# Moving the 8 KB buffer class of a two-block transformer kernel by 64 bytes

## The chip, the cores and the metric

The kernel runs on one core of a Trainium2 chip. The metric is the device time of one execution in microseconds; three runs of the kernel before gave 1069.27 us as median (1068.24 to 1070.73).

## The reference

Two transformer layers follow each other, with 512 tokens and 1024 features in float32. The first has a differential attention (4 heads) and a sparse attention with three branches (8 heads, 2 key-value heads): a compressed one, a selected one and a windowed one. The second has a short convolution, an attention over the 256 keys that an indexer picks, and a gated feed-forward layer (FFN) of width 2816.

```python
def reference(x, norm_g, w_in, ..., g_final_2):
    x = first_block(x, norm_g, w_in, ...)
    return second_block(x, g_mix_2, w_in_2, ...)

# second_block, its end
merged = gates[..., :D_MODEL] * y_a + gates[..., D_MODEL:] * y_b
x = x + merged @ w_out[layer]
h2 = rms_norm_2(x, g_ffn[layer])
x = x + (jax.nn.silu(h2 @ w_ffn_gate[layer]) * (h2 @ w_ffn_up[layer])) @ w_ffn_down[layer]
return rms_norm_2(x, g_final)
```

## The kernel before

Every dense product is made of three float32r matmuls: an operand is split into a rounded part and the rest (hi and lo), and hi by hi, hi by lo and lo by hi are summed in PSUM (`mm3`, line 169). A matmul reads two operands from SBUF: the stationary one is loaded into the array by a weight load (PEld in the profile), and the moving one is streamed through, 128 to 512 columns of 4 bytes per partition. The weight load of the next matmul overlaps the matmul before it. In the profile's names, `acc<-hT,whi` has hT as the moving and whi as the stationary operand.

The products come in two forms. In `gen_ii` and `gen_tt` a piece of the activation (hT, act, mg, oTd, oTn) is stationary and the weight moves, 256 to 512 columns at a time; in `gen_i` and in the FFN's first product (`Pair.product`) a piece of the weight is stationary and the activation moves (hT, yc, at with 512 columns, hA with 256). The FFN's first product is done with seven half-size products in place of eight (the sums `S1` to `S4` of the activations, and sums of the weights), and between these products a few steps of the second product are put (`feed_forward`, line 1416). Attention's dependent chains are spread out by due times (`defer`, `fill`), so that dense matmuls stand between the steps; the order of all instructions is written out when the program is built.

All tiles live in one SBUF pool. Each class of buffers (a tag, with a number of buffers) gets its room when its first tile is asked for, in that order, and each room is rounded up to 32 bytes per partition. The classes are `kf` (3 buffers of 4 KB), `k4` (13 of 4 KB), `k2` (19 of 2 KB), `k8` (13 of 8 KB), `sm` (28 of 96 bytes) and `kh` (4 of 512 bytes); a constant is a class of one buffer. Weights, raw and split, lie in `kf`, `k4` and `k2`, and so do probabilities, transposed probabilities and values; the activations that are operands of dense products, in hi and lo, lie in `k8`, and so do queries and keys, X, and the split weights of the first FFN products (`split_of` with `early`).

Four built-in constants and a 4 KB scratch area end at byte 4224, which is 16 x 256 + 128. `kf`, `k4` and `k2` follow (3 x 4096, 13 x 4096 and 19 x 2048 bytes), so that every buffer of theirs begins at 128 modulo 256. Then, before, come mhalf (32), identF (512), sm (28 x 96 = 2688), identR (512) and ones (32): 108672 + 3776 = 112448, which is 64 modulo 256. So every buffer of `k8` begins at 64 modulo 256, 64 bytes short of the phase of `k4` and `k2`; all pieces that a matmul reads lie at multiples of 512 bytes inside their buffer. identF, the identity that moves in transposes of float32, lies at 160 modulo 256, and identR, that of float32r, at 32.

```python
def t(self, cls, shape, dt=F32, name="w"):
    return self.pool.tile(shape, dt, name=name, tag=cls, bufs=BUFS[cls])

def const(self, shape, name, dt=F32):
    return self.pool.tile(shape, dt, name=name, tag="c_" + name, bufs=1)
```

Of the kernel before, what the change touches and what calls it, by code (L numbers as in the profile page):

```python
# [9 lines left out]
F32 = mybir.dt.float32  # L10
# [5 lines left out]
P = 128  # L16
# [31 lines left out]
class Kernel:  # L48
# [26 lines left out]
    def t(self, cls, shape, dt=F32, name="w"):  # L75
        return self.pool.tile(shape, dt, name=name, tag=cls, bufs=BUFS[cls])
# [104 lines left out]
    def tick(self):  # L181
        c, self.cost = getattr(self, "cost", 0.0), 0.0
        if self.filling and not self.busy:
            self.credit -= c
        self.spend(c)
# [66 lines left out]
def build(tc, pool, psum, dram, h):  # L252
    nc = tc.nc
    K = Kernel(tc, pool, psum, dram, h)
    t, ps, defer, tick = K.t, K.ps, K.defer, K.tick
# [15 lines left out]
    S, MAKE = Lazy(), {}  # L271
# [10 lines left out]
    def f32(ap):  # L282
        return ap.bitcast(F32)
# [108 lines left out]
    def new_hT():  # L392
        return [[t("k8", [P, 4, T], F32R, "hT") for _ in range(2)] for _ in range(2)]
# [26 lines left out]
        return f  # L420


    xin = [t("kf" if tt < 3 else "k4", [P, D], F32, "xt") for tt in range(NT)]
    gB1 = t("k4", [P, D], F32, "gB")

    def x_load(tt):
        for c in range(XP):
            a = slice(c * D // XP, (c + 1) * D // XP)
            S["x"] = tc.keep_in_program_order(nc.sync.dma_start(xin[tt][:, a], x[tt * P:(tt + 1) * P, a])).ins

    grow = t("k2", [P, P], F32, "grow")[0:8]
    nc.scalar.dma_start(grow, h["norm_g"][0].rearrange("(r c) -> r c", c=P))
    x_load(0)

    mhalf = K.const([P, 1], "mhalf")
    V.memset(mhalf, -0.5)
    identF = K.const([P, P], "identF")
    make_identity(nc, identF)
# [15 lines left out]
        K.tr(warm, gB1[:, b * P:(b + 1) * P], identF)  # L454
    identR = K.const([P, P], "identR", F32R)
    G.tensor_copy(identR, identF)
    ones = K.const([P, 1], "ones")
    V.memset(ones, 1.0)


    S["hT"] = new_hT()

    NV = 65
    maskc = K.const([P, T], "maskc")
    DM = K.const([P, T], "DM")
    cmask = K.const([P, 4, 32], "cmask")
    rowok = K.const([P, 1], "rowok")
    qsc = K.const([P, 4, 2, 4], "qsc")
    cw2 = K.const([P, 2, 2, 64], "cw2")
    rbT = K.const([8, 32], "rbT")  # L470
    rel_rows = dram.tile([8, 640], F32, name="rel_rows")
# [1 line left out]
    vec = K.const([P, NV], "vec")  # L473
    GD = K.const([P, 64], "GD")
    GN = K.const([P, 3, 64], "GN")
    c01 = K.const([P, 2], "c01")

    def constants():
        vrow = t("k2", [P, P], F32, "vrow")
# [337 lines left out]
        return evac  # L817


    KC = K.const([P, 64], "KC")  # L820

    def cmp_evac(m, o):
        v = m % 2
# [68 lines left out]
    def cmp_finish():  # L892
        for v in range(2):
# [5 lines left out]
            if v == 0:  # L899
# [12 lines left out]
                def go(kd=kd):  # L912
                    pk = ps([P, 64], name="pt")
                    K.tr(pk, kd[0:64].rearrange("p a d -> p (a d)"), identF[0:64, 0:64])
                    A.copy(KC, pk)
                    tick()
# [18 lines left out]
    def cmp_attention(g):  # L935
        st = {}

        def rows(tt):
            sc = ps([P, 4, 32], name="sc")
            for c in range(4):  # L940
                K.mm(sc[:, c, :], f32(S["nQ%d" % g][:, c, tt * P:(tt + 1) * P]), KC[:, g * 32:(g + 1) * 32],
                     c == 0, c == 3)
# [718 lines left out]
def emit(tc, h, stage="all"):  # L1661
    with tc.tile_pool(name="sb", bufs=1) as pool, \
            tc.tile_pool(name="ps", bufs=1, space=bass.MemoryType.PSUM) as psum, \
            tc.tile_pool(name="dr", bufs=1, space=bass.MemoryType.DRAM) as dram, \
            contextlib.nullcontext():
        build(tc, pool, psum, dram, h)
# [18 lines left out]
```

## Time and profile before

| | |
|---|---|
| median of three runs | 1069.27 us |
| the profiled execution | 1069.85 us |
| its span, first to last instruction | 1068.1 us |
| mean granted TensorE clock | 0.996 |
| matmuls / weight loads | 7251 / 7251 |
| PE, PEld busy | 1045.6 us (98%), 963.6 us (90%) |
| VectorE, ScalarE, GpSimd busy | 717.8, 556.2, 398.5 us |
| DMA, mean over the span | 103 GB/s |

The times of the profile are those of one execution. A matmul's recorded end is modelled and lies behind the start of the next one, so that the length of one matmul in a row says little, and a busy PE is not one that works at its peak. What can be read exactly is the start: the pitch, the time from the start of one matmul to the start of the next, is taken from two starts of the timeline and the number of matmuls between them. A few records of matmuls can be missing.

### The profile page before, as it was taken

How to read it: one execution, taken by the hardware profiler on the slowest of the kernel's cores; microseconds unless marked ns; L12 is line 12 of the kernel's file. 1: busy time of each engine (PE TensorE's matmuls, PEld its weight loads, DVE VectorE, ACT ScalarE, POOL GpSimd, SP SyncE). 2: the span in 40 equal slices, each digit the busy share in tenths (PEclk: the TensorE clock that was granted, in tenths of full speed). 3: DMA queues.
4: the chain of work that ended last, by engine and by line, in shares of the span. 5: the costliest groups of instructions: out<-in, count | busy, mean ns of one | idle time of the engine just before them, and what ended most of it. 6: DMA issues, size and time to landing. Idle time of an engine off the chain costs nothing.

```text
span 1068.1 us, 18962 instructions
## 1 busy us (share of the span) xinstructions
PE 1045.6 (98%) x7251; PEld 963.6 (90%) x7251; DVE 717.8 (67%) x1469; ACT 556.2 (52%) x1154; POOL 398.5 (37%) x403
## 2 busy tenths in 40 slices
PE   7999999999999999999999999999999999999997
PEld 6999898899789899888888888989999999999995
DVE  6777467346993637999313663979887777777724
ACT  5566687647883445523323776426444444444433
POOL 4442366465466231112015975910012112121241
PEclk9999999999999999999999999999999999999999
DMA  6446321221204434435331323651433323333122
GB/s 184 124 110 161 79 61 40 73 86 41 79 21 148 139 82 159 115 82 168 99 98 53 88 88 100 227 158 54 145 109 119 119 76 104 92 116 109 31 90 79
DMA packets 128085, 109.69 MB, mean 103 GB/s; under 512 B 20393, under 2 KB 119154, under 8 KB 127994
## 3 DMA queue, kind: packets, MB, share of 16 engines
q1 hardware_dynamic: 126906, 105.83, 33.8%
q0 software_dynamic: 1072, 2.65, 0.6%
q8 instruction: 57, 0.93, 0.4%
q14 instruction: 34, 0.28, 0.1%
q10 hardware_dynamic: 16, 0.00, 0.0%
HBM read 103.13 MB, written 6.84 MB: 103 GB/s over the span
## 4 chain that ended last, share of the span: by engine, by line
PE 88%; DVE 5%; DMA 2%; POOL 2%; ACT 2%; issue 1%; SPq 0%; POOLq 0%; DVEq 0%; ACTq 0%
PE acc L164 75%; PE pt L178 5%; PE sc L164 4%; PE o L164 4%; POOL wlo L208 1%; DMA xt<-in_x 1%; ACT p L637 1%; DMA raw<-in_w_ffn_up 1%; DVE p L635 1%; DVE acc L1550 0%; POOL mg L1214 0%; DVE mg L1217 0%; DMA raw<-in_w_out 0%; DVE wlo L208 0%; DVE hA L1402 0%
## 5 line engine op out<-in xcount | busy, mean ns | idle before, releaser
L208 POOL TENSOR_TENSOR wlo<-raw,whi 128x1024 fp32r<-128x1024 f32 (+4 forms) x99 | 205.1, 2077 | 443.5 <-ACT whi L206 343.7
L164 PE MATMUL acc<-hA,wh 128*128 128x256 f32 x1264 | 219.5, 280 | 1.8 <-ACT wh L1273 1.8
L206 ACT CAST whi<-raw 128x1024 fp32r<-128x1024 f32 (+4 forms) x143 | 131.9, 924 | 125.5 <-PE acc L164 80.1
L164 PE MATMUL acc<-hT,whi 128*128 128x512 f32 x608 | 194.4, 398 | 0.0
L164 PEld LDWEIGHTS acc<-hA,wh 128*128 128x128 f32 x1264 | 190.3, 190 | 2.4 <-ACT wh L1273 2.0
L164 PE MATMUL acc<-whi,hT 128*128 128x256 f32 (+3 forms) x896 | 181.2, 291 | 2.0 <-ACT whi L206 1.9
L164 PE MATMUL acc<-hA,wl 128*128 128x256 f32 x584 | 163.1, 280 | 0.0
L164 PEld LDWEIGHTS acc<-whi,hT 128*128 128x128 f32 x896 | 144.4, 189 | 3.3 <-ACT whi L206 2.2
L164 PEld LDWEIGHTS acc<-hT,whi 128*128 128x128 f32 x608 | 112.2, 188 | 24.5 <-ACT r L1549 0.2
L164 PE MATMUL acc<-wlo,hT 128*128 128x256 f32 (+3 forms) x448 | 129.4, 289 | 0.9 <-DVE wlo L208 0.9
L164 PE MATMUL acc<-whi,act 128*128 128x256 f32 (+1 forms) x640 | 130.0, 289 | 0.0
L164 PE MATMUL acc<-hT,wlo 128*128 128x512 f32 x304 | 120.9, 398 | 0.0
L164 PEld LDWEIGHTS acc<-hA,wl 128*128 128x128 f32 x584 | 110.3, 189 | 0.0
L164 PEld LDWEIGHTS acc<-whi,act 128*128 128x128 f32 x640 | 104.0, 188 | 2.5
L164 PE MATMUL acc<-wlo,act 128*128 128x256 f32 (+1 forms) x320 | 92.3, 289 | 0.0
L637 ACT ACTIVATE p<-p,s 128x128 f32<-128x128 f32 (+3 forms) x128 | 72.1, 565 | 32.0 <-DVE s L635 28.9
L1273 ACT CAST wh<-raw 128x1024 fp32r<-128x1024 f32 x55 | 57.6, 1051 | 55.2 <-PE acc L164 45.7
L164 PEld LDWEIGHTS acc<-wlo,hT 128*128 128x128 f32 x448 | 84.7, 189 | 1.4 <-DVE wlo L208 1.1
L1274 DVE TENSOR_TENSOR wl<-raw,wh 128x1024 fp32r<-128x1024 f32 x51 | 63.3, 1243 | 31.4 <-PE acc L164 17.3
L208 DVE TENSOR_TENSOR wlo<-raw,whi 128x1024 fp32r<-128x1024 f32 (+5 forms) x44 | 53.5, 1217 | 41.7 <-ACT whi L206 41.5
L164 PEld LDWEIGHTS acc<-hT,wlo 128*128 128x128 f32 x304 | 57.2, 188 | 13.1
L164 PEld LDWEIGHTS acc<-wlo,act 128*128 128x128 f32 x320 | 60.1, 188 | 1.3
(283 smaller groups left out, 2038.7 us busy)
## 6 DMA issues: line engine op xcount, KB each, us to landing
raw<-in_w_in SPq DMA_DIRECT2D x52, 512.0 KB, 3.9
raw<-in_w_ffn_gate SPq DMA_DIRECT2D x28, 512.0 KB, 3.9
raw<-in_w_ffn_up SPq DMA_DIRECT2D x22, 512.0 KB, 5.2
raw<-in_w_ffn_down SPq DMA_DIRECT2D x36, 256.0 KB, 5.3
raw<-in_w_out SPq DMA_DIRECT2D x16, 512.0 KB, 3.4
raw<-in_cmp_w SPq DMA_DIRECT2D x8, 512.0 KB, 3.7
raw<-in_w_in SPq DMA_DIRECT2D x10, 384.0 KB, 3.4
rel_all<-rel_rows POOLq DMA_DIRECT2D x1, 2560.0 KB, 17.2
```

Source lines behind the costliest of these rows:

```text
L164: self.nc.tensor.matmul(out, lhsT, rhs, start=start, stop=stop, skip_group_check=True)
L178: self.nc.tensor.transpose(out, in_, ident)
L206: self.nc.scalar.copy(hi, raw)
L208: (self.nc.gpsimd if every and self.split and self.split % every == 0 else self.nc.vector).tensor_tensor(lo, raw, hi.bitcast(F32), op=OP.s ...
L635: V.tensor_tensor_reduce(out=p[:, :n], in0=sc[:, :n], in1=bias, scale=-scale, scalar=3e38, op0=OP.add, op1=OP.min, accum_out=nm)
L637: S["exp"] = A.activation(p[:, :n], p[:, :n], AF.Exp, scale=-1.0, bias=nm, accum_out=z).ins
L1273: A.copy(hi, src)
L1274: eng.tensor_tensor(lo, src, f32(hi), op=OP.subtract)
```

## The change

Lines that ask for constants are put in another order, and `S["hT"]`, the first use of `k8`, is asked for earlier. Behind `k2` now comes `qsc` alone (4 x 2 x 4 floats, 128 bytes), then `k8`: 108672 + 128 = 108800, which is 0 modulo 256. So every buffer of `k8` begins at 0 modulo 256, 128 bytes from the phase of `k4` and `k2`, where it was 64. Behind `k8` come mhalf, ones, rowok, c01 (32 bytes each), KC (256), identF, sm and identR, and the constants that came later. identF now lies at 128 modulo 256, identR at 0, KC at 128 (32 before), the masks maskc, DM and cmask at 0 (64 before). `kf`, `k4`, `k2` and `kh` stay where they were.

No engine's sequence changes: each of the five has the same instructions with the same operands, waits and signals in the same order; only addresses in SBUF differ.

```diff
     xin = [t("kf" if tt < 3 else "k4", [P, D], F32, "xt") for tt in range(NT)]
     gB1 = t("k4", [P, D], F32, "gB")
+    grow = t("k2", [P, P], F32, "grow")[0:8]
+    qsc = K.const([P, 4, 2, 4], "qsc")
+    S["hT"] = new_hT()
+    mhalf, ones = K.const([P, 1], "mhalf"), K.const([P, 1], "ones")
+    rowok, c01 = K.const([P, 1], "rowok"), K.const([P, 2], "c01")
+    KC = K.const([P, 64], "KC")
...
-    grow = t("k2", [P, P], F32, "grow")[0:8]
     nc.scalar.dma_start(grow, h["norm_g"][0].rearrange("(r c) -> r c", c=P))
     x_load(0)
 
-    mhalf = K.const([P, 1], "mhalf")
     V.memset(mhalf, -0.5)
...
-    ones = K.const([P, 1], "ones")
     V.memset(ones, 1.0)
 
-
-    S["hT"] = new_hT()
...
-    rowok = K.const([P, 1], "rowok")
-    qsc = K.const([P, 4, 2, 4], "qsc")
...
-    c01 = K.const([P, 2], "c01")
...
-    KC = K.const([P, 64], "KC")
```

## Rows read from the trace of the kernel before

**Rows 1.** The page: busy time of each engine over the span with the number of instructions (its part 1), and the shares of the chain of work that ended last, by engine (its part 4).

```profile
PE 1045.6 (98%) x7251; PEld 963.6 (90%) x7251; DVE 717.8 (67%) x1469; ACT 556.2 (52%) x1154; POOL 398.5 (37%) x403
...
PE 88%; DVE 5%; DMA 2%; POOL 2%; ACT 2%; issue 1%; SPq 0%; POOLq 0%; DVEq 0%; ACTq 0%
```

**Rows 2.** Groups of instructions by line on PE, of the whole span: line, engine, operation, output<-moving operand, stationary operand, shape, count | busy us, mean ns of one (with its modelled end) | idle time before. Only the counts are used. In the names, whi and wlo are the two halves of a weight tile (4 KB class, or 2 KB class for the FFN's second product), wh and wl those of the FFN's first product, hT, hA, act, at, yc, mg and oTd are activations (8 KB class).

```profile
L164 PE MATMUL acc<-hA,wh 128*128 128x256 f32 x1264 | 219.5, 280 | 1.8 <-ACT wh L1273 1.8
...
L164 PE MATMUL acc<-hA,wl 128*128 128x256 f32 x584 | 163.1, 280 | 0.0
...
L164 PE MATMUL acc<-whi,act 128*128 128x256 f32 (+1 forms) x640 | 130.0, 289 | 0.0
...
L164 PE MATMUL acc<-wlo,act 128*128 128x256 f32 (+1 forms) x320 | 92.3, 289 | 0.0
...
L164 PE MATMUL acc<-whi,hT 128*128 128x256 f32 (+3 forms) x896 | 181.2, 291 | 2.0 <-ACT whi L206 1.9
...
L164 PE MATMUL acc<-wlo,hT 128*128 128x256 f32 (+3 forms) x448 | 129.4, 289 | 0.9 <-DVE wlo L208 0.9
...
L164 PE MATMUL acc<-whi,mg 128*128 128x256 f32 (+1 forms) x192 | 43.4, 318 | 0.5 <-DVE mg L1217 0.5
...
L164 PE MATMUL acc<-wlo,mg 128*128 128x256 f32 (+1 forms) x96 | 29.9, 317 | 0.1
...
L164 PE MATMUL acc<-whi,oTd 128*128 128x256 f32 x128 | 23.8, 281 | 0.0
...
L164 PE MATMUL acc<-wlo,oTd 128*128 128x256 f32 x64 | 17.8, 279 | 0.0
...
L164 PE MATMUL acc<-hT,whi 128*128 128x512 f32 x608 | 194.4, 398 | 0.0
...
L164 PE MATMUL acc<-hT,wlo 128*128 128x512 f32 x304 | 120.9, 398 | 0.0
...
L164 PE MATMUL acc<-at,whi 128*128 128x512 f32 x64 | 20.1, 395 | 0.0
...
L164 PE MATMUL acc<-at,wlo 128*128 128x512 f32 x32 | 12.5, 395 | 0.0
...
L164 PE MATMUL acc<-yc,whi 128*128 128x512 f32 x64 | 20.1, 396 | 0.0
...
L164 PE MATMUL acc<-yc,wlo 128*128 128x512 f32 x32 | 12.7, 396 | 0.0
...
L178 PE MATMUL pt<-identF,p 128*128 128x128 f32 x280 | 46.6, 275 | 1.3 <-POOL p L1024 0.8 <-DVE PTb L654 0.3
...
L178 PE MATMUL pt<-identF,xn 128*128 128x128 f32 x88 | 12.9, 287 | 1.3 <-DVE xn L1473 1.3
```

**Rows 3.** Timeline of PE in the FFN: start in us, length in us with the modelled end, engine, line, operation, names, shape, count. Between the first row and the second lie 24 matmuls, between the second and the third 12, then 24, then 18.

```profile
879.47 0.40 PE L164 MATMUL acc<-hA,wh 128*128 128x256 f32 x2
...
882.20 0.28 PE L164 MATMUL acc<-whi,act 128*128 128x256 f32 x1
...
883.56 0.40 PE L164 MATMUL acc<-hA,wh 128*128 128x256 f32 x2
...
886.39 0.28 PE L164 MATMUL acc<-whi,act 128*128 128x256 f32 x1
...
888.52 0.40 PE L164 MATMUL acc<-hA,wh 128*128 128x256 f32 x2
```

**Rows 4.** Timeline of PE, same columns, at the FFN's start, behind the last of the row blocks. Each row of acc<-hA,wl follows two matmuls of acc<-hA,wh; from the first row to the second there are thirteen such triples, 39 matmuls.

```profile
733.21 0.28 PE L164 MATMUL acc<-hA,wl 128*128 128x256 f32 x1
...
737.63 0.28 PE L164 MATMUL acc<-hA,wl 128*128 128x256 f32 x1
```

**Rows 5.** Timeline of PE, same columns: 48 matmuls in which the weight tile (wh) is of the 8 KB class too, and the 12 transposes behind them.

```profile
714.66 5.92 PE L164 MATMUL acc<-hA,wh 128*128 128x256 f32 x48
720.41 1.47 PE L178 MATMUL pt<-identF,xs 128*128 128x128 f32 x12
721.72 0.60 PE L178 MATMUL pt<-identF,xn 128*128 128x128 f32 x4
```

**Rows 6.** Timeline of PE, same columns, in the first projection: 256 columns of a weight move against a stationary piece of hT. From the first row to the second there are ten triples, 30 matmuls.

```profile
212.21 0.28 PE L164 MATMUL acc<-wlo,hT 128*128 128x256 f32 x1
...
215.74 0.28 PE L164 MATMUL acc<-wlo,hT 128*128 128x256 f32 x1
```

**Rows 7.** Timeline of PE, same columns, in the second block's projection: 512 columns of hT move against a stationary piece of a weight. From the first row to the second there are seven triples, 21 matmuls.

```profile
530.84 0.40 PE L164 MATMUL acc<-hT,wlo 128*128 128x512 f32 x1
...
535.74 0.39 PE L164 MATMUL acc<-hT,wlo 128*128 128x512 f32 x1
```

**Rows 8.** Timeline of PE, same columns, in the last product: 512 columns of a weight move against a stationary piece of act. From the first row to the second there are 30 matmuls.

```profile
1038.95 0.39 PE L164 MATMUL acc<-wlo,act 128*128 128x512 f32 x1
...
1045.82 0.39 PE L164 MATMUL acc<-wlo,act 128*128 128x512 f32 x1
```

**Rows 9.** Stretches of the span: bounds in us, length, PE busy and its matmuls, granted clock, DMA share and GB/s.

```profile
732.00:768.00 36.00, 34.20 (x284) 0.95 0.44 132
800.00:1000.00 200.00, 200.00 (x1729) 1.00 0.33 100
```

**Rows 10.** Groups of instructions by line on VectorE, of the whole span: an addition that reads PSUM and a tile of the 8 KB class (X), and one that reads PSUM and a tile of the 2 KB class (part).

```profile
L1074 DVE TENSOR_TENSOR X<-acc,X 128x512 f32<-128x512 f32 x56 | 37.9, 682 | 18.6 <-PE acc L164 18.3
...
L1348 DVE TENSOR_TENSOR gu<-acc,part 128x512 f32<-128x512 f32 x33 | 22.5, 683 | 3.9 <-ACT part L1343 2.8 <-PE acc L164 1.2
```

## Prediction, made before the changed kernel was run

> **What bounds the kernel now.** I read the page first: PE is busy for 1045.6 of 1068.1 us, and the chain of work that ended last is PE for 88% of its length, DVE for 5%, everything else for 7% [rows 1]. So the time is the number of matmuls times their pitch, and only what alters the pitch can alter it by much. Since no engine's sequence changes, what is to be asked is whether the pitch hangs on where operands lie. The second view is therefore the timeline of PE, read by starts alone, for the same shape with operands of different classes. Three things are to be seen there.
>
> First, matmuls of one shape do not have one pitch. 256 columns of hA (8 KB class) against a weight of the 4 KB class take (737.63 - 733.21)/39 = 113.3 ns in one stretch [rows 4]. In the middle of the FFN the same instructions take 2.73/24 = 113.8 ns in one product and 2.83/24 = 117.9 ns in the next; the steps of the second product between them keep the pace of the product ahead of them, 1.36/12 = 113.3 and 2.13/18 = 118.3 ns [rows 3]. PE waits for nothing there, the granted clock is 1.00, and 200 us of this hold 1729 matmuls, 115.7 ns each [rows 9], the middle of the two paces.
>
> Second, the one stretch in which both operands are of the 8 KB class, so begin at the same phase modulo 256, is the slowest of this shape: 5.75/48 = 119.8 ns [rows 5].
>
> Third, direction counts. With 512 columns, hT moving against a weight takes 4.90/21 = 233.3 ns [rows 7], a weight moving against act 6.87/30 = 229.0 ns [rows 8]. In the first the stationary operand lies 64 bytes behind the moving one (modulo 256), in the second 64 bytes ahead. With 256 columns and hT stationary the pitch is 3.53/30 = 117.7 ns [rows 6].
>
> My reading is that the stream of the moving operand and the load of the next weights get in each other's way in SBUF, at worst with equal phases, and by more or less at a distance of 64 depending on which of them is ahead. The trace of before has no steady stretch of dense matmuls at a distance of 128. So what follows is an extrapolation along the distance 0, 64, 128.
>
> **The change part by part.** The distance between the 8 KB class and the weights goes from 64 to 128, in both directions. I take the cleanest pace seen as the bound from below (113.3 ns for 256 columns, twice that, 226.6, for 512) and the equal-phase pace as the bound from above (119.8; 233.3 for 512, the slowest row). Counts are those of [rows 2].
>
> - 512 columns with the 8 KB class moving: 608 + 304 (hT) + 64 + 32 (at) + 64 + 32 (yc) = 1104, now at 233.3. At the nearest row that is better, 229.0, this gives 1104 x 4.3 = 4.7 us; at 226.6 it gives 7.4.
> - FFN, 256 columns: 1264 + 584 (hA) and 640 + 320 (act), of which 96 have 512 columns (the last product: 4 row blocks x 2 halves x 4 pieces x 3). Of the 2712 left, 284 are in the stretch that is clean already [rows 9], and 96 have weights of the 8 KB class, whose distance stays 0. 2332 x (115.7 - 113.3) = 5.6 us.
> - A weight moving against hT, mg or oTd: 896 + 448, 192 + 96 less 96 of 512 columns, 128 + 64, in all 1728 of 256 columns or a little more: 1728 x (117.7 - 113.3) = 7.6 us.
> - The 192 of 512 columns among act and mg: 192 x (229.0 - 226.6) = 0.5 us, or nothing.
> - Scores (query by key, both in the 8 KB class) and probabilities by values (both in the smaller classes) keep their distance 0: nothing.
>
> The sum lies between 17.9 and 21.1 us; I take 19.5. Not all of it arrives: where PE waits for a softmax chain or for a GpSimd subtraction, a faster PE waits longer. 12% of the chain is not PE's [rows 1], so I count 88%: 17.2 us.
>
> identF moves to the phase of p and xn, the data that its transposes load as weights: distance 0 where it was 32. The 280 + 88 transposes take 1.31/12 = 109.2 ns now (the same form, with xs) [rows 2, 5]. If they pay what the equal phase costs above, 119.8 - 113.3 = 6.5 ns, that is 2.4 us; since the trace shows no second distance for them, a gain of the same size can't be excluded. I take a third of the cost, 0.8 us.
>
> Other homes that change: X on VectorE. Its addition takes 682 ns with the 8 KB class at 64 and 683 with a tile of the 2 KB class at 128 [rows 10]; that engine doesn't mind, and I count masks and small tiles at nothing. Were VectorE slower by the same 5% as PE between its paces, it would still have a third of the span free.
>
> So 1069.85 - 17.2 + 0.8 = 1053.4 us for an execution like the profiled one. That one lay 0.6 above the median of the runs: 1053 us (rounded). The likeliest case by itself reaches from 1047 (all of 21.1 us and nothing lost) to 1058 (half of the third term and of the first missing).
>
> [...]
>
> **The rivals.**
>
> *Half of it: the two paces stay.* In the FFN the pace flips where the second product's steps give way to the next half-size product, with the same classes on both sides [rows 3]. So distance alone doesn't fix the pace; something that is carried along does, perhaps how far the weight load trails the stream. Then the 256-column matmuls may go on flipping at distance 128, and only hT, at and yc with 512 columns gain: 4.7 x 0.88 = 4.1 us, 1065. Against it: the flip comes just where the last weight that moves and the next stationary weight are both of the small classes, distance 0, and none comes within a product.
>
> *No effect.* Homes don't matter to PE, and the paces come from something else, such as what the other engines do meanwhile: 1069. For it: that the paces flip with homes unchanged. Against it: the 39 matmuls at 113.3 ns [rows 4] run beside VectorE and ScalarE work of the same kind, and the equal-phase stretch has no pace but 119.8.
>
> *Slower: the pattern repeats every 128 bytes.* Then a distance of 128 is a distance of 0, and all dense matmuls pay what the 48 of [rows 5] pay. Price: 2332 x (119.8 - 115.7) = 9.6; the 284 clean ones 284 x 6.5 = 1.8; 1728 x (119.8 - 117.7) = 3.6; the 192 of 512 columns 192 x (233.3 - 229.0) = 0.8; 15.8 us together, all of it on PE's chain: 1069.85 + 15.8 - 0.6 = 1085 us. For it: in the FFN the plus-64 and the minus-64 direction share one pace, fast or slow [rows 3], which a period of 128 would make equal by itself. Against it: with 512 columns the two directions differ, 233.3 against 229.0 [rows 7, 8], which it would not. It decides from the point at which products of hA against a 4 KB weight average more than 116 ns.
>
> **How the numbers follow.** The clean case 0.52, half of it 0.15, no effect 0.13, slower 0.20. About 0.2% is what a measurement of this kernel can tell from no change. Faster takes the first two, 0.67; within 0.2% 0.13; slower 0.20. The predicted time is that of the likeliest case, 1053 us. The range reaches from 1045 (the whole 21.1 us and a gain on the transposes) over the half case and no effect to 1076, the near half of the slower case, which leaves most of that case's 0.20 outside and little below. The clean case's own range is 1047 to 1058.
>
> **What would show it.** Right: in the FFN every product at 113 to 114 ns, so some 1760 matmuls between the bounds of 200 us where 1729 stand now [rows 9]; hT with 512 columns at 229 or less; the 48 matmuls with both operands of the 8 KB class still at 119.8 ns, since their distance is unchanged; VectorE's, ScalarE's and GpSimd's mean durations as before. A gain that is smaller with the paces as predicted would show as more idle time ahead of PE, behind softmax chains and GpSimd's wlo. The transposes of identF at 109 ns would put their term at nothing. Wrong: paces that still flip between 113 and 118 (half of it), the same mixture as before everywhere (no effect), or 119 to 120 for all of the FFN and no 512-column pitch under 233 (slower).

## The result and the profile after

The changed kernel is slower: 1077.51 us as median of four runs (1077.27 to 1077.77) against 1069.83 (1068.24 to 1070.73) for the kernel before in the same measurement, a ratio of 1.0076 with a 95% interval of 1.0060 to 1.0092. Forecast were 1053 us and a range of 1045 to 1076: the sign is wrong, and the time lies 1.5 us above the range.

The page of after, its busy times and its chain, which answer to [rows 1]:

```profile
span 1075.7 us, 18962 instructions
...
PE 1054.1 (98%) x7251; PEld 971.9 (90%) x7251; DVE 717.5 (67%) x1469; ACT 556.0 (52%) x1154; POOL 398.9 (37%) x403
...
PE 89%; DVE 5%; DMA 2%; ACT 2%; issue 1%; POOL 0%; SPq 0%; POOLq 0%; DVEq 0%; ACTq 0%
```

The span grew by 7.6 us and PE's busy time by 8.5, with the same 7251 matmuls; the other three engines have what they had, within 0.4 us. So the question is the pitch, and the matmuls of [rows 3 to 8] are looked up again. First the FFN, the same five matmuls as in [rows 3] (24, 12, 24 and 18 matmuls between them; columns as there):

```profile
882.93 0.28 PE L164 MATMUL acc<-hA,wh 128*128 128x256 f32 x1
885.79 0.28 PE L164 MATMUL acc<-whi,act 128*128 128x256 f32 x1
887.22 0.28 PE L164 MATMUL acc<-hA,wh 128*128 128x256 f32 x1
890.06 0.28 PE L164 MATMUL acc<-whi,act 128*128 128x256 f32 x1
892.20 0.28 PE L164 MATMUL acc<-hA,wh 128*128 128x256 f32 x1
```

2.86/24 = 119.2, 1.43/12 = 119.2, 2.84/24 = 118.3 and 2.14/18 = 118.9 ns. Before they were 113.8, 113.3, 117.9 and 118.3: the fast pace is gone, and the flipping with it. The stretch that was clean before [rows 4], 39 matmuls:

```profile
734.64 0.28 PE L164 MATMUL acc<-hA,wl 128*128 128x256 f32 x1
...
739.26 0.28 PE L164 MATMUL acc<-hA,wl 128*128 128x256 f32 x1
```

4.62/39 = 118.5 ns, where it was 113.3. Then the control, [rows 5]: operands of one class, and the transposes.

```profile
716.05 5.90 PE L164 MATMUL acc<-hA,wh 128*128 128x256 f32 x48
721.79 1.47 PE L178 MATMUL pt<-identF,xs 128*128 128x128 f32 x12
723.10 0.60 PE L178 MATMUL pt<-identF,xn 128*128 128x128 f32 x4
```

5.74/48 = 119.6 ns (119.8 before) and 1.31/12 = 109.2 (109.2 before): where the distance stayed, the pitch stayed, and identF's new home made no difference. Next the places of [rows 6], [rows 7] and [rows 8], with 30, 21 and 30 matmuls from the first row to the second of each pair:

```profile
212.57 0.28 PE L164 MATMUL acc<-wlo,hT 128*128 128x256 f32 x1
...
216.12 0.28 PE L164 MATMUL acc<-wlo,hT 128*128 128x256 f32 x1
...
532.24 0.40 PE L164 MATMUL acc<-hT,wlo 128*128 128x512 f32 x1
...
537.14 0.39 PE L164 MATMUL acc<-hT,wlo 128*128 128x512 f32 x1
...
1046.27 0.40 PE L164 MATMUL acc<-wlo,act 128*128 128x512 f32 x1
...
1053.24 0.39 PE L164 MATMUL acc<-wlo,act 128*128 128x512 f32 x1
```

3.55/30 = 118.3 ns (117.7 before), 4.90/21 = 233.3 (233.3) and 6.97/30 = 232.3 (229.0). Last the stretch of 200 us of [rows 9], with its columns, and VectorE's two additions of [rows 10]:

```profile
800.00:1000.00 200.00, 200.00 (x1688) 1.00 0.33 100
```

```profile
L1073 DVE TENSOR_TENSOR X<-acc,X 128x512 f32<-128x512 f32 x56 | 37.9, 682 | 19.5 <-PE acc L164 19.2
...
L1347 DVE TENSOR_TENSOR gu<-acc,part 128x512 f32<-128x512 f32 x33 | 22.5, 683 | 3.7 <-ACT part L1342 2.8 <-PE acc L164 0.9
```

1688 matmuls in place of 1729, 118.5 ns each in place of 115.7, at a granted clock of 1.00 in both. VectorE's addition takes 682 ns with X at either home. The delay can be followed by the starts of the same matmuls in the rows above and in those of before: 0.36 us at 212, 1.40 at 531, 1.43 at 733, 3.68 at 889, 7.32 at 1039 and 7.42 at 1046. Most of it arises in the FFN.

### The profile page after: what moved, and what is told of

Same layout as the page of the kernel before. It is cut to its first block, busy times and chain, and to the rows that moved or that the text cites. A ratio compares the mean times of both kernels' runs of the same rounds, so it can differ in the third digit from the quotient of the medians.

```text
span 1075.7 us, 18962 instructions
## 1 busy us (share of the span) xinstructions
PE 1054.1 (98%) x7251; PEld 971.9 (90%) x7251; DVE 717.5 (67%) x1469; ACT 556.0 (52%) x1154; POOL 398.9 (37%) x403
## 4 chain that ended last, share of the span: by engine, by line
PE 89%; DVE 5%; DMA 2%; ACT 2%; issue 1%; POOL 0%; SPq 0%; POOLq 0%; DVEq 0%; ACTq 0%
PE acc L164 77%; PE pt L178 5%; PE sc L164 4%; PE o L164 4%; DMA xt<-in_x 1%; ACT p L637 1%; DMA raw<-in_w_ffn_up 1%; DVE p L635 1%; DVE acc L1549 0%; DVE mg L1216 0%; DMA raw<-in_w_in 0%; DMA raw<-in_w_out 0%; DVE wlo L208 0%; SPq L437 0%; DVE hA L1401 0%
## 5 line engine op out<-in xcount | busy, mean ns | idle before, releaser
L164 PE MATMUL acc<-hA,wh 128*128 128x256 f32 x1264 | 223.0, 282 | 1.5 <-ACT wh L1272 1.5
L164 PE MATMUL acc<-whi,act 128*128 128x256 f32 (+1 forms) x640 | 132.7, 293 | 0.0
```

The costliest lines, as they stand in the source:

```text
L164: self.nc.tensor.matmul(out, lhsT, rhs, start=start, stop=stop, skip_group_check=True)
```

## Experiments

Below, a distance is the beginning of the moving operand less that of the stationary one, modulo 256. Before, hA, hT, at and yc against a weight of the 4 KB class have 192, and a weight that moves against act, hT, mg or oTd has 64; after, both have 128.

**Matmuls alone, by distance.** A kernel of its own: two tiles at phase 0, 48 matmuls of 256 columns or 24 of 512 in a row, at each distance in steps of 16.

```diff
+    def run(o, n, d, count, base=0, first=True):
+        for j in range(count):
+            w = wt[:, base + (j % 8) * 128:base + (j % 8) * 128 + 128]
+            m0 = base + d // 4 + (j % (1024 // n if n < 512 else 4)) * (n if n < 512 else 512)
+            nc.tensor.matmul(o[:, 0:n], w, mv[:, m0:m0 + n], start=first and j == 0, stop=j == count - 1,
+                             skip_group_check=True)
```

> A kernel of its own that leaves out the whole computation: stretches of 48 matmuls of 256 columns (24 of 512) whose moving operand begins 0, 16, ... 240 bytes past the stationary one, modulo 256, each behind an idle moment, and the 256-column ones once more behind 12 matmuls at distance 0 without an idle moment; three more shift both operands by 32, 64, 128 bytes at one distance (192). Theory one (the pitch hangs on the distance of the two streams): 119 to 120 ns at 0, 118 to 119 at 128, 113 to 118 at 64 and 192, and the three shifted stretches equal to the unshifted one at 192. Theory two (the phase of an operand by itself): one pitch at all distances within 1 ns, and the three shifted stretches differ from each other. Theory three (neither; PE does not mind homes): one pitch, about 113 ns, everywhere.

A row of its windows (PE, PEld, ACT and POOL busy, clock, DMA) shows that beside PE only ScalarE ran, in 34 short copies between the stretches; the rows of its timeline give a pitch each: the start of "end" or "pre" less that of the stretch ahead, over its count. a064q is 256 columns at distance 64 behind an idle PE, c192q at 192 behind 12 matmuls at distance 0 (pre), b000q 512 columns at 0 behind an idle PE.

```profile
20.00:350.00 330.00, 321.85 (x2270) 294.99 (x2269) 9.02 (x34) 0.00 (x0) 1.00 0.00 1
```

```profile
41.80 5.82 PE L37 MATMUL a064q<-mv,st 128*128 128x256 f32 x48
47.45 0.28 PE L47 MATMUL end<-mv,st 128*128 128x256 f32 x1
...
67.64 5.92 PE L37 MATMUL a128q<-mv,st 128*128 128x256 f32 x48
73.40 0.28 PE L47 MATMUL end<-mv,st 128*128 128x256 f32 x1
...
93.64 5.81 PE L37 MATMUL a192q<-mv,st 128*128 128x256 f32 x48
99.29 0.28 PE L47 MATMUL end<-mv,st 128*128 128x256 f32 x1
...
119.48 5.62 PE L37 MATMUL b000q<-mv,st 128*128 128x512 f32 x24
124.94 0.39 PE L47 MATMUL end<-mv,st 128*128 128x512 f32 x1
...
326.25 5.62 PE L37 MATMUL c192q<-mv,st 128*128 128x256 f32 x48
331.71 1.58 PE L37 MATMUL pre<-mv,st 128*128 128x256 f32 x12
```

5.65/48 = 117.7 ns at 64, 5.76/48 = 120.0 at 128, and at 192 5.65/48 = 117.7 behind an idle PE but 5.46/48 = 113.8 behind a dense stretch; 512 columns at 0 take 5.46/24 = 227.5. The pitches in ns at every second distance, from starts that are not rounded (a row's 0.01 us is 0.2 ns here):

| distance | 0 | 32 | 64 | 96 | 128 | 160 | 192 | 224 |
|---|---|---|---|---|---|---|---|---|
| 256 columns, behind idle | 120.0 | 116.8 | 117.9 | 119.9 | 120.0 | 117.4 | 117.7 | 118.2 |
| 256, behind 12 at distance 0 | 120.0 | 117.9 | 117.9 | 120.0 | 118.8 | 117.4 | 113.7 | 118.4 |
| 512 columns, behind idle | 227.4 | 232.9 | 229.1 | 234.1 | 233.1 | 234.1 | 233.6 | 233.2 |

Between these, 16 (113.5 or 118.8), 112 (114.4) and, with 512 columns, 240 (226.8) are fast. So PE's pitch does hang on the distance, with nothing running beside it; but not as the prediction had it. It isn't smooth, 192 isn't 64 the other way round, 128 isn't far from 0 for 256 columns, and for 512 columns the equal phase is among the fastest. At some distances there are two paces, at 192 for one 117.7 ns behind an idle PE and 113.7 behind a dense stretch, so that what came before has a part in it.

**One part of the change at a time.**

```diff
+    K.const([P, 48], "pad")
     S["hT"] = new_hT()
```

> The kernel before with 192 unused bytes ahead of the 8 KB class, which so begins at 0 modulo 256, 128 from the weights; identF, identR and the small tiles stay at their homes of before. Theory one: the pitch comes from the 8 KB class against the weights, so this is as slow as the changed kernel, 1077 us, with the FFN at 118 to 119 ns. Rival (the homes of identF, identR and the small constants): as before, 1069 to 1070 us.

This is the kernel before with 192 unused bytes ahead of the 8 KB class, so that only this class and what lies behind it moves: 1077.5 us, ratio 1.0074 (1.0051 to 1.0098), the whole loss. Its 8 KB class begins at byte 112640, that of the changed kernel at 108800. These are 3840 bytes apart, 15 x 256, and the time is the same: here the home modulo 256 is what counts.

```diff
+    K.const([P, 16], "pad0")
     S["hT"] = new_hT()
+    K.const([P, 48], "pad1")
```

> The changed kernel with 64 unused bytes ahead of the 8 KB class and 192 behind it: the 8 KB class is back at 64 modulo 256, every other tile keeps the phase of the changed kernel. Theory one: as before the change, 1069 to 1070 us, the FFN flipping between 113 and 118 ns. Rival (constants' homes): as the changed kernel, 1077 us.

This is the kernel after with the 8 KB class back at 64 and all else as after: 1069.16 us, ratio 1.0000 (0.9988 to 1.0011). The constants' homes made no difference.

```diff
+    K.const([P, 16], "pad")
     xin = [t("kf" if tt < 3 else "k4", [P, D], F32, "xt") for tt in range(NT)]
```

> The kernel before with 64 unused bytes ahead of all classes: weights begin at 192, the 8 KB class at 128 modulo 256, at the distance of before. Theory one (distance alone): 1069 to 1070 us, paces as before. Theory two (the phase of the 8 KB class by itself, 64 good, 0 and 128 bad): slower, towards 1077 us, with no pace of 113 ns.

All classes 64 bytes further, distances kept: 1068.63 us, ratio 0.9992 (0.9982 to 1.0002). Where in 256 bytes the pair lies made no difference for this shift; the distance did.

**What decides between two paces.** Again matmuls alone, first at distance 64, 128 and 192 behind nine kinds of stretches, then the FFN's alternation of its two forms.

```diff
+    for k8 in (64, 0, 192, 128, 32, 96, 160, 224):
+        reset(last)
+        for r in range(3):
+            for c, na in enumerate((24, 12, 24, 18)):
+                last = ps("f%03d%sq" % (k8, "ab"[c % 2]))
+                run(last, 256, *((128, k8) if c % 2 == 0 else (k8, 128)), na)
```

> The whole computation is left out: the run holds matmuls alone, with all other engines idle. First part: 48 matmuls of 256 columns at distance 64, 128 and 192 (moving operand behind the stationary one, modulo 256), each behind an idle PE and behind nine other stretches (256 columns at distance 0, 32, 64, 96, 128, 192; 512 columns at 0, 64, 192). Second part: the FFN's alternation without anything else: 24, 12, 24, 18 matmuls, three times, of the form weight stationary and activation moving and of the form activation stationary and weight moving in turn, weights at 128 modulo 256, activations at 64 (as before), 0 (as after), 192, 128, 32, 96, 160, 224. Theory (distance sets which patterns there are, the stretch ahead sets which of them runs): at 192 some preludes give 113.5 and others 117.7, with nothing between; at 128 120.0 or 118.7; at 64 117.9 always; in the second part activations at 64 show both 113 to 114 and 117 to 118 in turn, with a mean of 115 to 116.5, and activations at 0 118.5 to 120 in both forms. Rival (the distance alone sets the pace, and the flips of the kernel's FFN come from what VectorE, ScalarE and DMA do beside it): in the second part, where those engines are idle, each form keeps one pace all through, 117.7 to 117.9 for activations at 64, and no prelude matters.

Its timeline with the activations at 64, the homes of before (a: activation moves, b: weight moves):

```profile
246.53 2.90 PE L37 MATMUL f064aq<-mv,st 128*128 128x256 f32 x24
249.26 1.52 PE L37 MATMUL f064bq<-mv,st 128*128 128x256 f32 x12
250.62 2.99 PE L37 MATMUL f064aq<-mv,st 128*128 128x256 f32 x24
253.46 2.28 PE L37 MATMUL f064bq<-mv,st 128*128 128x256 f32 x18
255.58 2.90 PE L37 MATMUL f064aq<-mv,st 128*128 128x256 f32 x24
...
274.47 3.02 PE L37 MATMUL f000aq<-mv,st 128*128 128x256 f32 x24
...
283.74 3.00 PE L37 MATMUL f000aq<-mv,st 128*128 128x256 f32 x24
```

2.73/24 = 113.8, 1.36/12 = 113.3, 2.84/24 = 118.3 and 2.12/18 = 117.8 ns, and again from the start: these are the four numbers of [rows 3] to within 0.5 ns (from starts that are not rounded 113.8, 113.4, 118.0 and 117.9 in both), with all other engines idle, as the row of the windows shows (columns as above):

```profile
246.50:273.60 27.10, 27.10 (x235) 27.10 (x235) 0.00 (x0) 0.00 (x0) 1.00 0.01 1
```

The flips of the FFN come from PE's own order of work. With activations at 0, the homes of after, a round of 78 takes 9.27 us, 118.8 ns a matmul, as the changed kernel's FFN. In the first part 192 gave 113.3 to 113.8 behind seven of the nine dense stretches and 117.7 or 117.8 behind two (512 columns at 64 and 192), never anything between; behind all nine 64 gave 117.8 to 117.9 and 128 118.5 to 118.9. Behind an idle PE 192 had 113.6 this time, 117.7 in the sweep, so that an idle PE is no fixed start either (the two runs were on two chips, and no run separates that). The expectation that 64 has one pace only was wrong: in the alternation the fast stretch at 192 hands its pace on to the next one at 64 (the 12 at 113.3).

**The whole kernel at other distances.** The runs of matmuls alone now make forecasts. Two kernels move the 8 KB class only, to 192 and to 128; two move the 2 KB class (the weights of the FFN's second product) to 0 and leave the 8 KB class at 192 or at 64.

```diff
+    K.const([P, 32], "pad")
     S["hT"] = new_hT()
```

> Whole kernel, 8 KB class at 192 modulo 256: hA, hT, at, yc moving at distance 64, weights moving at 192. Theory (pitches by distance as the runs of matmuls alone gave them, 88% of their sum): hT, at, yc with 512 columns go from 233.3 to 229.0 ns, 1104 x 4.3 = -4.7 us; a weight moving against hT, mg, oTd (1728) stays at 117.7 or falls to 113.5, 0 to -7.3 us, as the stretch ahead decides; the 192 of 512 columns go from 229.0 to 233.7, +0.9; the FFN's alternation gave 116.0 with activations at 192 and 115.9 at 64, so nothing there. Sum -11.1 to -3.8, times 0.88: 1060 to 1066 us where the kernel before has 1069 to 1070, so faster than both kernels. Rival (64 bytes ahead or behind is one and the same in a whole kernel, only the distance's size counts): 1069 to 1070.

1064.7 us (1063.91 to 1065.72, five runs), ratio 0.9967 (0.9954 to 0.9980): faster than both kernels, and inside the forecast. Its stretch of 200 us in the FFN, and two matmuls 21 apart, the ones of [rows 7]:

```profile
800.00:1000.00 200.00, 200.00 (x1729) 1.00 0.31 96
```

```profile
526.80 0.39 PE L164 MATMUL acc<-hT,wlo 128*128 128x512 f32 x1
...
531.61 0.39 PE L164 MATMUL acc<-hT,wlo 128*128 128x512 f32 x1
```

The FFN is where it was, 1729 matmuls, since the two forms have only changed places; hT with 512 columns takes 4.81/21 = 229.0 ns in place of 233.3. By the starts of all its matmuls that group of 608 + 304 gained 3.2 us of the 5.7 by which the span fell between the two profiled executions (to 1062.4), at and yc 0.8, weights of 256 columns against hT, mg and oTd 2.8; weights of 512 columns against act, mg and oTn lost 1.9, where 0.9 was forecast.

```diff
+    K.const([P, 16], "pad")
     S["hT"] = new_hT()
```

> Whole kernel, 8 KB class at 128 modulo 256, so that all classes have the same phase, distance 0. Theory: all 256-column products at 120.0 (the FFN from 115.7 and 113.3, 1752 x 4.7 + 864 x 4.3 = +11.9 us; weights moving 1728 x 2.3 = +4.0), 512 columns at 226.7 to 227.4 (1104 x -6.3 = -7.0, 192 x -2 = -0.4): +8.5, times 0.88 = +7.5 us, some 1077 us. The FFN's 200 us would hold 200/0.120 = 1667 matmuls. Rival (the reading of the prediction, equal phases slowest for every shape): 512 columns at 233.3 or more, +15 us, 1084 us.

1077.06 us (1076.83 to 1077.47), ratio 1.0081 (1.0066 to 1.0096); 1669 matmuls in the 200 us, 119.8 ns each, where 1667 were forecast:

```profile
800.00:1000.00 200.00, 200.00 (x1669) 1.00 0.33 100
```

It has the time of the changed kernel for another reason: 256 columns are slower still, 512 columns take 227 to 228 ns. The two matmuls of [rows 7], 21 apart, show it, 4.76/21 = 226.7 ns:

```profile
531.51 0.39 PE L164 MATMUL acc<-hT,wlo 128*128 128x512 f32 x1
...
536.27 0.39 PE L164 MATMUL acc<-hT,wlo 128*128 128x512 f32 x1
```

```diff
+    K.const([P, 32], "pad2")
     grow = t("k2", [P, P], F32, "grow")[0:8]
```

> Whole kernel, 2 KB class at 0 and 8 KB class at 192 modulo 256, 4 KB class at 128: as the run with the 8 KB class at 192, except that the weights that move against act (2 KB class) are at distance 64 as in the kernel before. Theory: the FFN loses its fast pace, since distance 64 has only 117.9: hA 1752 x 2.6 = +4.6, act 864 x 2.2 = +1.9; hT, at, yc -4.7; weights moving against hT, mg, oTd 0 to -7.3; 512 columns of the rest +0.9. Sum -4.6 to +2.7, times 0.88: 1065 to 1072 us, slower than the run with the 8 KB class alone at 192. Rival (the stretch ahead, not the distance, sets the FFN's pace): as that run.

1069.24 us, ratio 1.0003 (0.9994 to 1.0013), 4.5 us slower than with the 8 KB class alone at 192, as forecast. With both of its forms at 64, the FFN has no fast stretch to take the pace from, and none shows one: 1700 matmuls, 117.6 ns each.

```profile
800.00:1000.00 200.00, 200.00 (x1700) 1.00 0.32 97
```

```diff
+    K.const([P, 32], "pad2")
     grow = t("k2", [P, P], F32, "grow")[0:8]
...
+    K.const([P, 32], "pad")
     S["hT"] = new_hT()
```

> Whole kernel, 2 KB class moved to 0 modulo 256, the 8 KB class at 64 and the 4 KB class at 128 as before: both of the FFN's forms at distance 192, the one with two patterns (113.5 and 117.8). All other dense products as before. Theory: whichever pattern a product starts in stays, so that the FFN is anywhere between all at 113.5 (1752 x -1.8 + 864 x -2.2 = -5.0 us) and all at 117.8 (+6.2); 1065 to 1075 us; which one, the stretches between the products decide, and the trace is to show one or both of these two paces and nothing between. Rival (paces flip by themselves, whatever the distance): as before, 1069 to 1070.

1071.03 us, ratio 1.0025 (1.0014 to 1.0036). The five matmuls of [rows 3] once more:

```profile
880.29 0.28 PE L164 MATMUL acc<-hA,wh 128*128 128x256 f32 x1
883.12 0.29 PE L164 MATMUL acc<-whi,act 128*128 128x256 f32 x1
884.50 0.28 PE L164 MATMUL acc<-hA,wh 128*128 128x256 f32 x1
887.32 0.29 PE L164 MATMUL acc<-whi,act 128*128 128x256 f32 x1
889.39 0.28 PE L164 MATMUL acc<-hA,wh 128*128 128x256 f32 x1
```

2.83/24 = 117.9, 1.38/12 = 115.0, 2.82/24 = 117.5 and 2.07/18 = 115.0 ns. Behind the first four matmuls of a stretch, which still settle, nearly all products of hA run at 117.8 and all but one of act at 113.3 or 113.4. Both forms have distance 192, so the distance doesn't decide. The form alone doesn't either: with the 8 KB class at 192, where act is at distance 192, its products have both paces, 113.3 and 117.7. What fits is the stretch ahead, which here is the same each time; this run alone doesn't show it. The time says little, since the range of 1065 to 1075 reaches past that of the rival on both sides.

**Own weights or the next ones.** The last run asks which distance counts, that to a matmul's own weights or that to the next ones: the weights' phase is shifted by 128 from one matmul to the next, the moving operand with it.

```diff
+                        s = k % 2 * alt
+                        w0, m0 = s // 4 + k % 8 * 128, (s + d) // 4 + k % (1024 // n if n < 512 else 4) * n
```

> The whole computation is left out: matmuls alone again, 48 of 256 columns or 24 of 512, behind an idle PE and behind 12 at distance 0. Each matmul's moving operand lies 0, 64, 128 or 192 bytes (modulo 256) behind its own weights; in one half of the stretches all weights have one phase, in the other half weights and moving operand both shift by 128 from matmul to matmul, so that the distance to the own weights stays and that to the next weights is 128 more. Theory (the stream of a matmul and the load of the next weights, which runs beside it, get in each other's way, as the prediction reads it): the shifting stretches have the pitch of the distance to the next weights: own 0 as 128 (118.5 to 120 and 233), own 64 as 192 (113.4 or 117.8, and 233.5 with 512 columns), own 128 as 0 (120.0 and 227), own 192 as 64 (117.8 and 229). Rival (what counts is the distance of a matmul's two operands themselves): shifting changes nothing, with 512 columns 227, 229, 233 and 233.5 for own 0, 64, 128 and 192 in both halves.

```profile
23.92 5.92 PE L62 MATMUL g256d000a000pq<-mv,st 128*128 128x256 f32 x48
29.68 0.28 PE L47 MATMUL end<-mv,st 128*128 128x256 f32 x1
...
38.32 5.77 PE L62 MATMUL g256d000a128pq<-mv,st 128*128 128x256 f32 x48
43.92 0.28 PE L47 MATMUL end<-mv,st 128*128 128x256 f32 x1
```

Without the shift (a000) distance 0 gives 5.76/48 = 120.0 ns, with it (a128) 5.60/48 = 116.7; shifted stretches have 116.7 to 117.1 with 256 columns whatever their own distance, and with 512 columns 228.5 or 228.7 (own 0) and 230.0 to 230.3 (own 64, 128, 192). Neither reading holds: the pitch follows neither the own nor the next weights alone. What inside the chip makes it so is not shown.

## Why the prediction was wrong

**What bounds the kernel, and that the homes set the pitch** was right. PE's pitch is all that changed, and the run with the 8 KB class alone moved gives the whole difference. Why the homes do so was a reading only, the stream against the load of the next weights; the run that shifts own and next weights apart did not bear it out (116.7 ns where 118.5 to 120 were expected of it).

**The step that failed is the extrapolation "along the distance 0, 64, 128"**, which took the cleanest pace seen, 113.3 and 226.6 ns, for a distance that no row showed. Measured at 128: 118.3 to 119.2 ns in the dense work of 256 columns, 232.3 and 233.3 with 512. Its ground, "at worst with equal phases", holds for 256 columns only, with 120.0 ns at 0; with 512 the equal phase is among the fastest, 227.4 ns in the run of matmuls alone and 227 to 228 in the whole kernel with all classes at one phase. And the two sides of 64 are two distances, 64 and 192, with paces of their own, so that the rows of before were no two points on one line.

Term by term, the change of all start-to-start times of each group between the two traces:

| term | predicted, us | measured, us |
|---|---|---|
| 512 columns, 8 KB class moving | -4.7 to -7.4 | -0.5 |
| FFN, 256 columns (hA, act) | -5.6 | +5.9 |
| weight moving against hT, mg, oTd, 256 to 320 columns | -7.6 | +1.5 |
| weight moving against act, mg, 512 columns | -0.5 or 0 | +0.4 |
| weight moving against oTn, 512 columns | not counted | +0.3 |
| same class on both sides | 0 | -0.1 |
| identF's transposes of p and xn | +0.8 | -0.1 |
| VectorE and other engines | 0 | 0 |

These make 7.4 of the 7.65 us by which the last start moved. Another 0.15 are 64 products of a weight with At, which no term counts. The 96 products of oTn were overlooked, with a price as small as their number. Of the 1728 of the third term 480 have 264 to 320 columns, "or a little more", and changed by 0.1 us in all: 46 of 320 columns take 6.75 us, 146.7 ns each, before (373.86 to 380.61 us) and after (375.26 to 382.01). So next to nothing of 480 x 4.4 = 2.1 us of that term could arrive. PE's idle time fell from 22.5 to 21.6 us (span less busy time), so that little of the slower pitch disappeared in waits; the factor of 0.88, meant for a gain, found no test here.

**The rivals.** "Slower" had the direction, the place and its test right (hA's products average 118.6, above 116), but its mechanism wrong: with a period of 128 bytes 64 and 192 would be equal, and so would 0 and 128; the run of matmuls alone has 117.9 and 113.7, and 227.4 and 233.1 with 512 columns. Its price, 119.8 for everything, is twice what came: 15.8 us against 7.6. The range ended at the near half of that case, at 1076, just short of what came. "Half of it" saw rightly that something carried along fixes the pace beside the distance, which the alternation of matmuls alone then showed; but at 128 the FFN shows no fast pace to flip to (118.3 to 119.2 ns). "No effect" falls with the run that moves the 8 KB class alone, ratio 1.0074. With PE alone at work one shape has 113.3 to 120.0 ns by the distance of its operands and by what came before. Which part of the chip makes the difference no run here shows.

## What to carry to other kernels

Where PE sets the time, the homes of its two operands relative to each other (modulo 256 bytes) were worth up to 6% of the pitch with 256 columns here (113.3 to 120.0 ns), up to 3% with 512 (226.7 to 234.1) and nothing with 320 (146.6 to 146.7); measure each pair and shape that the kernel uses in a small kernel of matmuls alone, in the order of the real work, before any buffer is moved. A distance that no row shows has no price: put both ends of the paces seen on it, and both signs. Here the runs of matmuls alone forecast four whole kernels, each within its range or 1 us of the single time named (two of the ranges held the time of the kernel before as well), and one of them, the 8 KB class at 192 by 128 unused bytes, beat both kernels by 0.33% and 1.2%.

## What was not expected of the hardware

- Distance 192 has two steady paces, 113.3 and 117.8 ns, and behind dense work the stretch ahead decided which; 12 matmuls in between were enough to flip it (113.8 to 118.3 ns), and the granted clock is 1.00 in both.
- At 128 the changed kernel shows no steady pitch: from 884 us on, its FFN repeats rounds of five starts, about 115, 118, 122, 120 and 119 ns apart. Their mean, 118.8 ns, is what the sweep of matmuls alone has at 128 behind 12 matmuls at distance 0.
- 256 and 512 columns are fastest at different distances: 0 is among the slowest for one (120.0, as at 80 and 96) and among the fastest for the other (226.7 once settled, as at 240). With 320 columns the whole kernels have 146.6 to 146.7 ns at 0, 64, 128 and 192. With 512 columns 64 has two paces too, 5.51/24 = 229.6 behind an idle PE and 5.60/24 = 233.3 behind 12 matmuls of distance 0 (the run that shifts the weights, its stretches without a shift).
- No effect of the absolute phase was seen: three shifts of both tiles at distance 192 gave 113.6 to 113.8 ns, and the whole kernel shifted by 64 bytes had its old time. In the same run the pair without a shift had 117.7, its other pace, and 113.6 in the next run.
- Not tried: homes at steps of 16 bytes in a whole kernel, and classes split by use, so that 256 and 512 columns could each have a distance of their own.
